# Rows of seven experts through DRAM and indirect DMA, in a two-layer decoder with top-2 experts

## The chip, the core and the metric

The kernel runs on one core of a Trainium2 chip, in one launch. The core's engines run side by side, each with its own queue of instructions in program order, and wait for each other by semaphores: TensorE multiplies matrices, VectorE and ScalarE work on rows and read TensorE's sums, GpSimd is a slower engine for the same kind of work, and SyncE does little but issue DMA transfers. The metric is the device time of one execution in microseconds, lower is better; 1471.25 us is the median of three runs before the change.

## What is computed

Two decoder layers over 256 tokens of 1024 numbers, in fp32. Each has a set of attention heads and then a feed-forward part: dense in layer 0, and in layer 1 two of eight experts for each token. A final RMSNorm ends it. The change lies in the experts and in the norm behind them:

```python
def _moe_swiglu(h, router, w1, w3, w2):
    logits = (xt @ router).astype(jnp.float32)
    top_v, top_i = lax.top_k(logits, TOP_K)            # TOP_K = 2 of 8 experts
    gates = jax.nn.softmax(top_v, axis=-1)
    ...
    def body(args):
        tok, g, e = args
        xb = xt[tok]                                   # the tokens of expert e
        y = (jax.nn.silu(xb @ w1[e]) * (xb @ w3[e])) @ w2[e]     # 1024 -> 3584 -> 1024
        return y * g[:, None].astype(y.dtype)
    ...
    out = jnp.zeros((t, d), h.dtype).at[row_tok].add(...)
...
x = x + _moe_swiglu(rmsnorm(x, ffn_norm[1]), ...)
return rmsnorm(x, final_norm)
```

## The kernel before

**Weights.** All weights come as one stream of 1 MB units, 128 rows of 2048 numbers (`Stream`). SyncE loads a unit into the next free buffer (`raw`); ScalarE copies each half (a piece) rounded to the matmul's format (`wh`, L305), VectorE computes the rest (`wl`, L306), and TensorE multiplies with both, so that a product is three matmuls (`mm3`, L454 to L456). Five split pieces of either kind exist; `split_to` keeps the splitting four pieces ahead of TensorE in the expert stage (`MAHEAD`). A buffer is loaded again once VectorE has split its second piece. Tiles of other stages are added as buffers when they are free (`widen`), and some are taken back (`retire`).

**Order.** The expert stage is written out by hand: each engine does its work in the order of the code. `get` hands out a split piece, splits the one four ahead and runs what was put off by `defer(n)` to the n-th piece from there.

**Routing.** `moe` transposes the token rows with TensorE (`natural`) and keeps them as a rounded part and a rest (`xnh`, `xnl`). From the router's products come rank, mask and `pos`, the place of each token among the tokens of each expert. 128 slots belong to an expert; if one has more tokens than that, a second pass follows the first, which the data here don't need.

**Experts.** `experts` runs 8 experts in 7 steps (e, j) of 512 hidden columns. A step is `g1` (two products with w1 and w3, bank `acc`) and `g2` of the step before (product with w2, bank `mm`); between them TensorE transposes the hidden tile `hd` in four pieces (`hidden`). Twelve pieces are used in a step. Around the steps stands what moves tokens to slots and back, all of it on TensorE with a one-hot matrix `oh` (slot by token):
- `gather`: 32 matmuls of 128x128 per expert, in step 5 of the expert before, in two groups; `gathered` takes them out of the bank with the norm's gains, in a rounded part (ScalarE) and a rest (VectorE).
- `back`: in step 6, two transposes of `oh` to `sT`, and the slots' 1/rms by two fp32 matmuls.
- `scatter`: in step 1 of the next expert, eight matmuls of 128x512 from `sT` and the two parts of the expert's output (`yh`, `yl`); `put` adds them to the token rows `x`, times the gate, on VectorE.

**The end.** `Final` norms the rows; its gains are spread over the 128 partitions by 16 small matmuls with 8 rows (`gains`, L1147), which TensorE does in the last step.

## Time and profile before

| what | value |
|---|---|
| median of the runs (lowest, highest) | 1471.25 us (1470.4, 1471.53) |
| the profiled execution, its span | 1470.91 us, 1468.7 us |
| TensorE busy | 1448.2 us, 99% |
| VectorE busy | 1225.0 us, 83% |
| ScalarE busy | 1047.2 us, 71% |
| GpSimd busy | 31.8 us, 2% |
| bytes moved | 426.36 MB, 290 GB/s over the span |
| the expert stage | from about 462 us to the end |

Busy time says how long an engine had an instruction in work, and matmuls overlap, so that 99% of TensorE's time is not 99% of its peak. The average hides stages too: in the expert stage VectorE and the DMA engines are much fuller than over the whole span. Times in the rows are counted from the span's start.

### The profile page before, as it was taken

To read this page: it belongs to the slowest core of one execution; us is meant where nothing else is said; L and a number is where in the kernel's file an instruction comes from. 1 tells how busy PE (TensorE), PEld (TensorE's weight loads), DVE (VectorE), ACT (ScalarE), POOL (GpSimd) and SP (SyncE) were. 2 spreads that over 40 slices of the span, in tenths; PEclk is the share of its full clock that TensorE was granted. 3 is DMA by queue.
4 is the path that set the end of the run, shared out by engine and by line. 5 is a ranking of instruction groups with operands and counts; after the bars stand their busy time and mean duration, and the time that the engine had idled before them with its cause. 6 is when DMAs were issued, how large, how long until landed. Compare 5 with 4: busy or idle time off the path is not lost.

```text
span 1468.7 us, 21467 instructions
## 1 busy us (share of the span) xinstructions
PE 1448.2 (99%) x8092; PEld 1253.7 (85%) x8092; DVE 1225.0 (83%) x1574; ACT 1047.2 (71%) x1387; POOL 31.8 (2%) x38
## 2 busy tenths in 40 slices
PE   9999999999999999999999999999999999999996
PEld 7999999999997888888888888888888888888885
DVE  6766656666756998999999999899999999989995
ACT  6665544455755877887877878778887877878884
POOL 2001000001000010000000000000000000000000
PEclk9999999999998999999999999999999999999998
DMA  9723555457437988999999999999999999999770
GB/s 367 297 87 121 189 183 177 154 192 249 142 145 292 358 319 321 357 371 339 355 362 366 346 358 360 343 359 365 347 361 354 378 332 355 372 346 358 247 254 31
DMA packets 62334, 426.36 MB, mean 290 GB/s; under 512 B 7176, under 2 KB 7824, under 8 KB 13712
## 3 DMA queue, kind: packets, MB, share of 16 engines
q1 hardware_dynamic: 62224, 424.92, 78.5%
q8 instruction: 65, 1.06, 0.3%
q14 instruction: 45, 0.37, 0.1%
HBM read 423.85 MB, written 1.05 MB: 289 GB/s over the span
## 4 chain that ended last, share of the span: by engine, by line
PE 96%; DVE 1%; ACT 1%; issue 1%; DMA 1%; SPq 0%; POOL 0%; ACTq 0%; DVEq 0%; POOLq 0%
PE acc L454 14%; PE acc L456 14%; PE acc L455 14%; PE mm L454 7%; PE mm L455 7%; PE mm L456 7%; PE B L972 3%; PE B L971 3%; PE B L970 3%; PE A L522 2%; PE A L523 2%; PE A L524 2%; PE tp L1187 2%; PE tp L1239 2%; PE A L594 2%; PE A L595 1%
## 5 line engine op out<-in xcount | busy, mean ns | idle before, releaser
L306 DVE TENSOR_TENSOR wl<-raw,wh 128x1024 fp32r<-128x1024 f32 (+2 forms) x801 | 966.8, 1224 | 140.9 <-ACT wh L305 103.5
L305 ACT ACTIVATE wh<-raw 128x1024 fp32r<-128x1024 f32 (+2 forms) x801 | 844.5, 1057 | 282.5 <-PE acc L456 105.3
L454 PE MATMUL acc<-wh,g 128*128 128x512 f32 x896 | 357.1, 399 | 0.0
L455 PE MATMUL acc<-wl,g 128*128 128x512 f32 x896 | 350.0, 391 | 0.4 <-DVE wl L306 0.4
L456 PE MATMUL acc<-wh,g 128*128 128x512 f32 x896 | 350.1, 391 | 0.0
L456 PEld LDWEIGHTS acc<-wh,g 128*128 128x128 f32 x896 | 168.6, 188 | 36.7
L455 PEld LDWEIGHTS acc<-wl,g 128*128 128x128 f32 x896 | 168.9, 189 | 33.6 <-DVE wl L306 0.9
L454 PEld LDWEIGHTS acc<-wh,g 128*128 128x128 f32 x896 | 168.6, 188 | 32.9
L454 PE MATMUL mm<-wh,th 128*128 128x512 f32 x440 | 171.9, 391 | 0.0
L455 PE MATMUL mm<-wl,th 128*128 128x512 f32 x440 | 171.7, 390 | 0.0
L456 PE MATMUL mm<-wh,tl 128*128 128x512 f32 x440 | 171.6, 390 | 0.0
L456 PEld LDWEIGHTS mm<-wh,tl 128*128 128x128 f32 x440 | 82.9, 188 | 17.6 <-DVE tl L460 0.3
L455 PEld LDWEIGHTS mm<-wl,th 128*128 128x128 f32 x440 | 82.9, 188 | 17.4
L454 PEld LDWEIGHTS mm<-wh,th 128*128 128x128 f32 x440 | 82.9, 188 | 17.3
L972 PE MATMUL B<-xh,wl 128*128 128x256 f32 x336 | 95.2, 283 | 0.0
L970 PE MATMUL B<-xh,wh 128*128 128x256 f32 x336 | 95.1, 283 | 0.0
L971 PE MATMUL B<-xl,wh 128*128 128x256 f32 x336 | 95.1, 283 | 0.0
L970 PEld LDWEIGHTS B<-xh,wh 128*128 128x128 f32 x336 | 64.5, 192 | 0.0
L971 PEld LDWEIGHTS B<-xl,wh 128*128 128x128 f32 x336 | 64.5, 192 | 0.0
L972 PEld LDWEIGHTS B<-xh,wl 128*128 128x128 f32 x336 | 64.5, 192 | 0.0
L594 PE MATMUL A<-xh,wh 128*128 128x256 f32 x176 | 51.4, 292 | 0.0
L595 PE MATMUL A<-xl,wh 128*128 128x256 f32 x176 | 49.7, 283 | 0.0
(256 smaller groups left out, 1749.3 us busy)
## 6 DMA issues: line engine op xcount, KB each, us to landing
raw<-in_wmoe SPq DMA_DIRECT2D x324, 1024.0 KB, 6.9
raw<-in_wt SPq DMA_DIRECT2D x53, 1024.0 KB, 4.8
raw<-in_wmoe SPq DMA_DIRECT2D x24, 512.0 KB, 5.3
ac<-in_att SPq DMA_DIRECT2D x2, 1728.0 KB, 8.8
raw<-in_wt SPq DMA_DIRECT2D x5, 512.0 KB, 4.8
raw<-in_wt SPq DMA_DIRECT2D x2, 960.0 KB, 16.1
raw<-in_wt SPq DMA_DIRECT2D x2, 928.0 KB, 8.4
raw<-in_wt SPq DMA_DIRECT2D x2, 832.0 KB, 8.8
```

The lines of the kernel that those rows point to most:

```text
L305: nc.scalar.activation(h[:, sl], raw[:, sl], AF.Copy)
L306: nc.vector.tensor_sub(l[:, sl], raw[:, sl], h[:, sl].bitcast(F32))
L454: pe.matmul(o, lh, rh, start=start, stop=False, **kw)
L455: pe.matmul(o, lh, rl, start=False, stop=False, **kw)
L456: pe.matmul(o, ll, rh, start=False, stop=stop, **kw)
L522: pe.matmul(o, wh[wsl], h, start=s0, stop=False, skip_group_check=True)
L523: pe.matmul(o, wh[wsl], lo, start=False, stop=False, skip_group_check=True)
L594: pe.matmul(o, hv[:, k], xh[:, k], start=k == 0, stop=False)
L595: pe.matmul(o, hv[:, k], xl[:, k], start=False, stop=False)
L970: pe.matmul(o, hv[:, k], xh[:, k], start=k == 0, stop=False)
L971: pe.matmul(o, hv[:, k], xl[:, k], start=False, stop=False)
L972: pe.matmul(o, lv[:, k], xh[:, k], start=False, stop=k == KC - 1)
```

## The change

Experts 1 to 7 get their tokens by another way, and the outputs of experts 0 to 6 go back by another way; expert 0 still gathers with matmuls, and expert 7 still scatters with them.

- **There.** The token rows `xx`, now in plain fp32, are multiplied by the norm's gains on GpSimd and written to DRAM (`x_out`, `x_rows`, 1 MB). For each expert two fp32 matmuls of the one-hot with two columns (`numbers`) give each slot's token number and 1/rms; GpSimd clears a tile and fetches the slots' rows by an indirect DMA with these numbers (`fetch`). TensorE turns the fetched rows with eight transposes (`turn`), which are split on their way out of the bank (`turned`).
- **Back.** ScalarE copies an expert's output to a tile that GpSimd writes to DRAM (`put`, `y_rows`, 512 KB). In step 1 of expert 7 GpSimd clears two tiles and fetches for each token the rows of its two places (`collect`, four indirect DMAs of 512 KB); a token with no place in experts 0 to 6 gets nothing by the bounds check. VectorE adds them, times the shares, in steps 3 and 4 of expert 7 (`add`). The places and shares come from `places`, 15 small VectorE instructions in step 1 of expert 0.
- **Else.** Gains of the MoE norm and of the final norm are loaded as rows spread over the partitions, so `Final.gains` and its matmuls go. One weight buffer more (`more`) stays to the end, and `oTh`, `oTl` are taken back at step 5 of expert 6. The two parts `xnh`, `xnl` and their subtractions go.

```diff
-ONCE = ("g1", "yy", "xx")
-RETIRE = {1: "g1", 2: "xx", 3: "yy"}
+ONCE = ("g1", "yy")
+RETIRE = {1: "g1", 3: "yy"}
+FAR = 4096.0
...
-        st.widen([big_slot("oTh"), big_slot("oTl")])
+        for tag in ("oTh", "oTl"):
+            st.widen([big_slot(tag)], tag)
         for tag in ONCE:
             st.widen([mp_slot(tag)], tag)
+        st.widen([mp_slot("more")])
+        row = mp.tile([128, D], F32, name="row")
+        nc.sync.dma_start(row, bcast(P_MOE, D))
...
-        def natural_x():
-            xx = mp.tile([128, 2, D], F32, name="xx")
+        def x_out():
+
             for t in range(2):
-                x.append(xx[:, t])
-                pool.tensor_add(x[t], xnh[t].bitcast(F32), xnl[t].bitcast(F32))
-
+                xg = mp.tile([128, D], F32, name="xg")
+                pool.tensor_mul(xg, x[t], row)
+                pool.dma_start(x_rows[128 * t:128 * t + 128], xg)
+
+        x_out()
...
-            def gains(self, c):
-                for i in range(4):
-                    pe.matmul(self.gf[c][:, 128 * i:128 * i + 128],
-                              ident[0:8, 4 * c + i:4 * c + i + 1].to_broadcast([8, 128]), self.gfin, start=True, stop=True)
...
                 p = bank()
-                for v in (xnh, xnl):
-                    for c, k in enumerate(ks):
-                        for t in range(2):
-                            pe.matmul(p[:, 128 * c:128 * c + 128], v[t][:, 128 * k:128 * k + 128], self.oh[t],
-                                      start=v is xnh and c == t == 0, stop=v is xnl and k == ks[-1] and t == 1,
-                                      skip_group_check=True)
+                for c, k in enumerate(ks):
+                    for t in range(2):
+                        pe.matmul(p[:, 128 * c:128 * c + 128], x[t][:, 128 * k:128 * k + 128], self.oh[t],
+                                  start=c == t == 0, stop=k == ks[-1] and t == 1, skip_group_check=True)
...
+            def numbers(self):
+                self.p = tp()
+                for t in range(2):
+                    pe.matmul(self.p[:, 0:2], self.oh[t], num[:, t], start=t == 0, stop=t == 1)
+
+            def numbered(self):
+                self.rsl = ms.tile([128, 1], F32, name="rsl", bufs=2)
+                self.who = ms.tile([128, 1], I32, name="who", bufs=2)
+                dve.tensor_scalar(self.who, self.p[:, 0:1], FAR, None, op0=ALU.add)
+                dve.tensor_copy(self.rsl, self.p[:, 1:2])
+
+            def fetch(self):
+
+                self.xg = mp.tile([128, D], F32, name="xg")
+                pool.memset(self.xg, 0.0)
+                pool.indirect_dma_start(self.xg, None, x_rows, bass.IndirectOffsetOnAxis(ap=self.who, axis=0),
+                                        bounds_check=S - 1, oob_is_err=False)
+
+            def turn(self, q):
+                self.p = tp()
+                for c in range(4):
+                    pe.transpose(self.p[:, 128 * c:128 * c + 128],
+                                 self.xg[:, 512 * q + 128 * c:512 * q + 128 * c + 128], ident)
...
-                    for c in range(2):
-                        sl = slice(512 * c, 512 * c + 512)
-                        st.defer(1 + c, lambda sl=sl, c=c: split_evac(yh[:, sl], yl[:, sl], Y[e][c]))
+                    ys = mp.tile([128, D], F32, name="yy")
+
+                    def put(c):
+                        act.activation(ys[:, 512 * c:512 * c + 512], Y[e][c], AF.Copy)
+                        if c == 1:
+                            pool.dma_start(y_rows[128 * e:128 * e + 128], ys)
+                    for c in range(2):
+                        st.defer(1 + c, lambda c=c: put(c))
...
+            def collect():
+
+                for t in range(2):
+                    yg.append(big.tile([128, 2, D], F32, name="yg", tag=("oTh", "oTl")[t]))
+                    pool.memset(yg[t], 0.0)
+                    for r in range(2):
+                        pool.indirect_dma_start(yg[t][:, r], None, y_rows,
+                                                bass.IndirectOffsetOnAxis(ap=take[:, r, t:t + 1], axis=0),
+                                                bounds_check=(E - 1) * 128 - 1, oob_is_err=False)
+
+            def add(t, r):
+                dve.scalar_tensor_tensor(x[t], yg[t][:, r], share[:, r, t:t + 1], x[t], op0=ALU.mult, op1=ALU.add)
...
-                if e and j == 1:
-                    for k in range(4):
-                        (b if k < 2 else c)[(0, 2, 0, 2)[k]] = [later(scatter, e - 1, k // 2, [k % 2], 1)]
...
+                if (e, j) == (E - 1, 1):
+                    c[1] = [collect]
+                if e == E - 1 and j in (3, 4):
+                    for r in range(2):
+                        (b, c)[r].setdefault(1, []).append(later(add, j - 3, r))
+                if half == 0 and (e, j) == (E - 2, 5):
+                    st.retire("oTh")
+                    st.retire("oTl")
...
-                if e + 1 < E and j == 4:
+                if e + 1 < E and j == 1:
                     st.defer(1, later(prepare, e + 1))
+                if e + 1 < E and j == 2:
+                    b[0] = [lambda: (G[e + 1].numbers(),
+                                     st.defer(1, lambda: (G[e + 1].numbered(), G[e + 1].fetch())))]
                 if e + 1 < E and j == 5:
                     for q in range(2):
-                        ks = list(range(4 * q, 4 * q + 4))
-                        b[2 * q] = [later(lambda ks: (G[e + 1].gather(ks, tp),
-                                                      st.defer(1, later(G[e + 1].gathered, ks))), ks)]
-                if e + 1 < E and j == 6:
+                        b[2 * q] = [later(lambda q: (G[e + 1].turn(q), st.defer(1, later(G[e + 1].turned, q))), q)]
+                if e == E - 2 and j == 6:
                     b[0] = [lambda: (G[e + 1].back(), st.defer(1, G[e + 1].backed))]
```

Three places show it in the order of the instructions. First TensorE in step 1 of expert 1, where a half of the scatter of expert 0 stood (`acc` and `mm` are the banks of the products, `tp` the bank for transposes, `g`, `th`, `tl` the slots' tokens and the hidden tile). Before:

```order
L455 MATMUL acc<-wl,g 128x512
L456 MATMUL acc<-wh,g 128x512
L1292 MATMUL tp<-yy,sT 128x512 x2
L454 MATMUL acc<-wh,g 128x512
L455 MATMUL acc<-wl,g 128x512
```

After the change, in step 5 of expert 0, where 16 gather matmuls stood in a row:

```order
L458 MATMUL acc<-wl,g 128x512
L459 MATMUL acc<-wh,g 128x512
L1250 MATMUL tp<-cst,xg 128x128 x4
L457 MATMUL acc<-wh,g 128x512
L458 MATMUL acc<-wl,g 128x512
```

The scatter's rows have gone without a row in their place, and a group of 16 gather matmuls has become one row of four transposes of the fetched tile.

Second, VectorE at the end of step 5 of expert 0 (`wl` are the splits of weights, `hd` and `tl` belong to the hidden tile, `g` are the rests of the gathered tokens). Before:

```order
L460 TENSOR_TENSOR tl<-tp,th 128x512
L306 TENSOR_TENSOR wl<-raw,wh 128x1024
L1199 SCALAR_TENSOR_TENSOR g<-tp,gains,g 128x128 x4
L306 TENSOR_TENSOR wl<-raw,wh 128x1024 x2
L1199 SCALAR_TENSOR_TENSOR g<-tp,gains,g 128x128 x4
L306 TENSOR_TENSOR wl<-raw,wh 128x1024
L1261 SCALAR_TENSOR_TENSOR hd<-acc,rsl,sg 128x512
```

After:

```order
L463 TENSOR_TENSOR tl<-tp,th 128x512
L309 TENSOR_TENSOR wl<-raw,wh 128x1024
L463 TENSOR_TENSOR g<-tp,g 128x512
L309 TENSOR_TENSOR wl<-raw,wh 128x1024 x2
L463 TENSOR_TENSOR g<-tp,g 128x512
L309 TENSOR_TENSOR wl<-raw,wh 128x1024
L1310 SCALAR_TENSOR_TENSOR hd<-acc,rsl,sg 128x512
```

Four instructions of 128x128 have become one of 128x512, twice, at the same place among the splits.

Third, GpSimd from the routing to the first experts (`rs_r` is the 1/rms, `xx` the token rows, `fm` the final norm's). Before, this is all that it does to the end of the kernel:

```order
L450 TENSOR_TENSOR rs_r<-rs_m,half 128x2
L1111 TENSOR_TENSOR xx<-xnh_5394,xnl_5396 128x1024
L1111 TENSOR_TENSOR xx<-xnh_5395,xnl_5397 128x1024
L1165 TENSOR_TENSOR fm<-fm,half 128x1 x2
L1371 TENSOR_LOAD cmaxi
```

After, up to the second expert's fetch:

```order
L453 TENSOR_TENSOR rs_r<-rs_m,half 128x2
L1119 TENSOR_TENSOR xg<-xx,row 128x1024
L1120 DMA x_rows<-xg 128x1024
L1119 TENSOR_TENSOR xg<-xx,row 128x1024
L1120 DMA x_rows<-xg 128x1024
L1243 MEMSET xg 128x1024
L1244 DMA xg<-x_rows,who 128x1024
L1332 DMA y_rows<-yy 128x1024
L1243 MEMSET xg 128x1024
L1244 DMA xg<-x_rows,who 128x1024
```

Clear, fetch and write-out repeat for each expert, seven times in all, in one queue.

## Rows read from the trace of the kernel before

**Rows 1.** The page: the span, and the chain that ended last by engine.
```profile
span 1468.7 us, 21467 instructions
...
PE 96%; DVE 1%; ACT 1%; issue 1%; DMA 1%; SPq 0%; POOL 0%; ACTq 0%; DVEq 0%; POOLq 0%
```

**Rows 2.** Table by stretches: start of the stage, a plain step, one expert.
```profile
core 0: us, PE busy (x) PEld busy (x) DVE busy (x) ACT busy (x) POOL busy (x), PEclk, DMA share, GB/s
462.00:482.00 20.00, 19.44 (x87) 15.81 (x87) 14.56 (x23) 16.34 (x20) 0.00 (x0) 0.94 0.78 262
...
587.00:604.00 17.00, 17.00 (x79) 14.00 (x78) 16.21 (x16) 14.47 (x17) 0.00 (x0) 1.00 1.00 374
...
710.00:833.00 123.00, 123.00 (x576) 102.31 (x575) 114.89 (x115) 98.60 (x109) 0.00 (x0) 1.00 0.97 357
```

**Rows 3.** Waits of SyncE's queue, then ScalarE's largest: total us, times, longest.
```profile
SPq L292 <- DVE wl L306: 792.8, 317, 9.2
...
ACT wh L305 <- PE acc L456: 78.5, 247, 0.8
```

**Rows 4.** The chain that ended last, steps around expert 1: start us, us, what.
```profile
551.21 1.73 PE tp L1187 x16
...
569.81 0.44 PE tp L1239 x4
...
571.87 0.34 PE tp L1207 x4
...
587.30 0.44 PE tp L1239 x4
...
604.12 0.44 PE tp L1239 x4
...
605.95 0.47 PE tp L1292 x2
...
622.75 0.44 PE tp L1239 x4
```

**Rows 5.** The same chain at the first gather group of expert 7.
```profile
1294.34 1.73 PE tp L1187 x16
```

**Rows 6.** The same chain in the last step, around the final gains.
```profile
1437.78 1.98 PE acc L1147 x16
...
1443.62 0.43 PE mm L455
...
1444.29 0.23 PE mm L454
```

**Rows 7.** Table by stretches: behind the final gains, and the gather of expert 0.
```profile
1440.50:1444.00 3.50, 3.50 (x10) 2.72 (x9) 2.05 (x3) 1.06 (x1) 0.00 (x0) 0.51 0.00 0
...
455.00:460.00 5.00, 4.74 (x23) 4.77 (x23) 3.03 (x12) 2.05 (x8) 0.70 (x1) 0.50 1.02 429
```

**Rows 8.** The chain in the gather of expert 0.
```profile
457.20 1.71 PE mm L1187 x8
```

**Rows 9.** VectorE's groups from 710 to 833 us, by shape: busy us, mean ns.
```profile
L1296 DVE SCALAR_TENSOR_TENSOR xx<-tp,gate,xx 128x512 f32<-128x512 f32 x4 | 3.0, 746 | 0.0
...
L1199 DVE SCALAR_TENSOR_TENSOR g<-tp,gains,g 128x128 fp32r<-128x128 f32 x8 | 2.3, 343 | 1.0 <-ACT g L1197 1.0
...
L460 DVE TENSOR_TENSOR yy<-mm,yy 128x512 fp32r<-128x512 f32 x2 | 1.4, 684 | 0.0
```

**Rows 10.** Order in time, VectorE before and during GpSimd's additions: start us, us.
```profile
491.48 9.16 DVE L306 TENSOR_TENSOR wl<-raw,wh 128x1024 fp32r<-128x1024 f32 x8
...
506.85 14.28 DVE L306 TENSOR_TENSOR wl<-raw,wh 128x1024 fp32r<-128x1024 f32 x8
...
513.15 5.76 POOL L1111 TENSOR_TENSOR xx<-xnh,xnl 128x1024 f32<-128x1024 f32 x2 [56.14 <-DVE wl L306]
```

**Rows 11.** DMA issues of the expert weights: count, KB each, us to landing.
```profile
raw<-in_wmoe SPq DMA_DIRECT2D x324, 1024.0 KB, 6.9
...
raw<-in_wmoe SPq DMA_DIRECT2D x24, 512.0 KB, 5.3
```

**Rows 12.** Order in time, one of VectorE's tiny instructions in `gates`.
```profile
478.31 0.17 DVE L1123 TENSOR_REDUCE gmx<-gate 128x2 f32<-128x16 f32 x1
```

**Rows 13.** Table by stretches: 5 us with a queue of loads to work off.
```profile
540.00:545.00 5.00, 5.00 (x24) 4.14 (x23) 5.00 (x6) 4.11 (x4) 0.00 (x0) 1.00 1.01 428
```

More of the change, by code (lines that the diff above doesn't have):

```diff
@@ L1098, in moe @@
         rs = rsqrt(ss, D, 2)
+        num = ms.tile([128, 2, 2], F32, name="num")
+        dve.tensor_copy(num[:, :, 0], ids[:, 0:2])
+        dve.tensor_copy(num[:, :, 1], rs[:, 0:2])
         cmax = ms.tile([128, 1], F32, name="cmax")
@@ L1125, in gates, with places @@
             dve.tensor_tensor(gate, gate, gm[:, 1, :, None].to_broadcast([128, 2, E]), op=ALU.mult)
+        take = ms.tile([128, 2, 2], I32, name="take")
+        share = ms.tile([128, 2, 2], F32, name="share")
+        def places():
+            n = E - 1
+            w = [ms.tile([128, 2, n], F32, name=f"pl{i}") for i in range(3)]
+            sm = ms.tile([128, 2, 2], F32, name="plm")
+            dve.tensor_tensor(w[0], pos[:, :, :n], ids[:, None, 2:2 + n].to_broadcast([128, 2, n]), op=ALU.add)
+            dve.tensor_scalar(w[1], pos[:, :, :n], -0.5, None, op0=ALU.is_gt)
+            dve.scalar_tensor_tensor(w[1], pos[:, :, :n], 127.5, w[1], op0=ALU.is_lt, op1=ALU.mult)
+            for r in range(2):
+                dve.scalar_tensor_tensor(w[2], rank[:, :, :n], float(r), w[1], op0=ALU.is_equal, op1=ALU.mult)
+                g = ms.tile([128, 2, n], F32, name="plg", bufs=2)
+                dve.tensor_mul(g, w[2], gate[:, :, :n])
+                dve.tensor_reduce(share[:, r], g, AX, ALU.add)
+                dve.tensor_mul(w[2], w[2], w[0])
+                dve.tensor_reduce(sm[:, r], w[2], AX, ALU.add)
+            far = ms.tile([128, 2, 2], F32, name="plf")
+            dve.tensor_scalar(far, sm, 0.5, FAR, op0=ALU.is_lt, op1=ALU.mult)
+            dve.scalar_tensor_tensor(take, sm, -1.0, far, op0=ALU.add, op1=ALU.add)
         psx.close()
@@ L1135, in moe, with __init__ @@
         class Final:
-            def __init__(self, gfin):
-                self.gfin = gfin
-                self.gf = [acc() for c in range(2)]
+            def __init__(self):
                 self.ss = ms.tile([128, 4], F32, name="fss")
@@ L1177, in __init__, with place @@
                 self.oh = oh or onehot(e)
-                both = mp.tile([128, 2, KC, 128], F32R, name="g", tag=f"g{e % 2}")
+                self.tag = f"g{e % 2}"
+            def place(self):
+                both = mp.tile([128, 2, KC, 128], F32R, name="g", tag=self.tag)
                 self.gh, self.gl = both[:, 0], both[:, 1]
@@ L1202, in back, with turned @@
+            def turned(self, q):
+                if q == 0:
+                    self.place()
+                split_evac(self.gh[:, 4 * q:4 * q + 4], self.gl[:, 4 * q:4 * q + 4],
+                           self.p.rearrange("p (c t) -> p c t", c=4))
             def back(self):
-                p = tp()
+                self.p = tp()
                 for t in range(2):
-                    pe.transpose(p[:, 128 * t:128 * t + 128], self.oh[t].bitcast(F32), ident)
-                for t in range(2):
-                    pe.matmul(p[:, 256:257], self.oh[t].bitcast(F32), rs[:, t:t + 1], start=t == 0, stop=t == 1)
@@ L1304, in prepare @@
                 G[e] = Slots(e)
+            yg = []
+            def collect():
[8 more added lines that the diff above has]
+                dve.scalar_tensor_tensor(x[t], yg[t][:, r], share[:, r, t:t + 1], x[t], op0=ALU.mult, op1=ALU.add)
             G[0] = Slots(0, oh0 if half == 0 else None)
-            for i in range(4):
-                ks = [2 * i, 2 * i + 1]
-                G[0].gather(ks, (tp, mm)[i % 2])
-                G[0].gathered(ks)
             if half == 0:
-                st.defer(8, gates)
+                G[0].place()
+                for i in range(4):
+                    ks = [2 * i, 2 * i + 1]
+                    G[0].gather(ks, (tp, mm)[i % 2])
+                    G[0].gathered(ks)
+                st.defer(8, gates)
+                st.defer(12, places)
+            else:
+                places()
+                G[0].numbers()
+                G[0].numbered()
+                G[0].fetch()
+                for q in range(2):
+                    G[0].turn(q)
+                    G[0].turned(q)
             for i, (e, j) in enumerate(steps):
@@ L1341, in experts @@
                     st.ahead = TAHEAD
-                    fin = Final(gfin)
-                    b[2] = [later(fin.gains, 0), later(fin.gains, 1)]
+                    fin = Final()
+                    fin.row = final_row
                     c[1] = [later(hidden, e, j)]
```

60 lines of the change are left out of this document (26 added, 34 removed).

## The prediction

> **What bounds the kernel now.** I read the page first: of the chain that ended last, 96% is TensorE work [rows 1]. Next, the table by stretches, for the expert stage. Over one expert (710 to 833 us) TensorE is busy for all 123.00 us, VectorE for 114.89, ScalarE for 98.60, and the DMA engines have a share of 0.97 at 357 GB/s [rows 2]. Three of the four are near full, so the question is which of them waits for which. The waits tell: SyncE, which issues the weight loads, stood 792.8 us waiting for VectorE's split of an earlier piece, that is, for a free buffer; and the waits of ScalarE, the first reader of a weight, are for TensorE to release a split buffer, with no row that names a DMA (the largest is shown) [rows 3]. So loads run ahead of use, and TensorE sets the pace, with VectorE some 7% behind it. What leaves TensorE's queue is worth its full length, until VectorE or the loads become the limit.
>
> How long things take on TensorE I read from the chain, where a row's length is the distance to the next. A step of the expert loop begins with four transposes of the hidden tile. A plain step lasts 604.12 - 587.30 = 16.82 us; the step with the way back (`back`) 587.30 - 569.81 = 17.49; the step with the scatter 622.75 - 604.12 = 18.63; a group of 16 gather matmuls takes 1.73, and there are two per expert [rows 4]. From the first group of expert 1, at 551.21, to that of expert 7, at 1294.34, are six experts: a period of 123.9 us [rows 4, 5].
>
> **The change on TensorE.** *Gather, experts 1 to 7.* Twice 1.73 us go. In their place stand twice four transposes of the fetched rows, the same operation and shape as the hidden tile's four, 0.44 [rows 4]. Saved: 2 x (1.73 - 0.44) = 2.58 an expert, 7 x 2.58 = 18.1 us.
>
> *Scatter, experts 0 to 6.* Eight matmuls go and nothing replaces them on TensorE: 18.63 - 16.82 = 1.81 an expert, 7 x 1.81 = 12.7 us. Expert 7 keeps its own.
>
> *`back`.* It costs 17.49 - 16.82 = 0.67, of which the two fp32 matmuls with one column (four records, so an fp32 matmul is two) are 0.34 [rows 4]. They stay, with two columns, as `numbers`; the two transposes stay for expert 7 alone. I take 0.23 an expert for them, 7 x 0.23 = 1.6 us.
>
> *Final gains.* Sixteen matmuls of 1.98 us go, and more with them: behind them the chain has nine 512-column matmuls at 0.43 us where one at full clock takes 0.23 [rows 6], and the granted clock is 0.51 in that stretch, which is the level of 1.2 GHz [rows 7]. These sixteen, with 8 of the 128 rows in use, are all that TensorE did differently before it fell, so I let the loss go too: 1.98 + 9 x 0.20 = 3.8 us (bounds 2.0, if the clock falls for another reason, and 3.8).
>
> *Gather of expert 0.* It stays on TensorE, as 16 fp32 matmuls. At two records each these are 32, as many as the 32 now, which take 1.71 us for eight [rows 8] with the clock at 0.50 [rows 7]. I take no difference; an fp32 record could cost half or one and a half times as much, so the bounds are -3.4 and +3.4 of its 6.8 us.
>
> Sum: 18.1 + 12.7 + 1.6 + 3.8 = 36.2 us less on TensorE; 2.58 + 1.81 + 0.23 = 4.6 us an expert make the period 119.2 instead of 123.9.
>
> **What hides the rest, and what it costs.** *VectorE.* It loses the four adds of the scatter (3.0 us an expert), the rests of `yy` (1.4) and the eight rests of the gather (2.3) [rows 9], and gains two 128x512 rests (1.4, the form of `yy`) and two tiny ones: 114.89 x 123.9 / 123 - 6.7 + 1.7 = 110.7 of the new 119.2. It stays behind TensorE, with 8.5 us an expert to spare.
>
> *GpSimd* was nearly empty; now it clears a tile, starts an indirect fetch and writes the outputs out, for every expert. No row shows a clear or a transfer of GpSimd's. The nearest are its two 128x1024 additions, 5.76 us together; while they ran, eight of VectorE's splits took 14.28 us, where eight took 9.16 a step earlier: VectorE lost 5.1 us [rows 10]. Per expert the bounds are then nothing and three such operations, 3 x 5.1 / 2 = 7.7 us of VectorE, which fits into the 8.5. I take nothing, since two of the three only start transfers and the third has no input. The Trainium skill ("SBUF — State Buffer", SBUF: two separate sides) says that a VectorE instruction with two inputs in SBUF contends with a GpSimd instruction that reads SBUF; these rows agree (splits with two inputs, an addition that reads, 5.1 us lost), and by it the clear, which reads nothing, would cost nothing, which no run here shows. The sum is the same by both.
>
> *Waiting for the fetch.* Expert e + 1 gets its numbers in the second half of step 2 of expert e; its rows are turned in the second half of step 5: 3 x 16.82 = 50 us in between. TensorE's next work is queued in order behind the turn, so a late fetch would stop everything. A 1 MB weight load lands 6.9 us after issue [rows 11] and a GpSimd operation is about 2.9; fetch, with half a megabyte, I put at 10 to 15 us. Hidden by 35.
>
> *The start.* Two multiplications on GpSimd (`x_out`) replace the two additions, but now while the first weights of the stage are split, and `places` puts 15 tiny VectorE operations, some 0.17 us each by the like one of `gates` [rows 12], 2.6 us, into the second step. 5.1 + 2.6 = 7.7 us more there; VectorE has 20 - 14.56 = 5.4 us free between 462 and 482 [rows 2]. What is over, 2.3 us, I charge as 2 (bounds 0 and 7.7, all of it exposed).
>
> *The end.* Four additions of 128x1024 on VectorE in steps 3 and 4 of expert 7, about twice 746 ns each [rows 9], 6 us, replace 28 of half that size earlier. VectorE has 17 - 16.21 = 0.8 us free in a plain step [rows 2], and splits run four pieces ahead of TensorE, 12 pieces to 16.82 us, that is 5.6 us. I take 0 (bounds 0 and 4).
>
> *The load path.* Weights are 324 x 1024 + 24 x 512 KB [rows 11] = 352.3 MB, 44.0 MB an expert. Two half-megabyte trips per expert add 1.05: 45.1 MB in 119.2 us, 378 GB/s. A plain step ran at 374 at a share of 1.00 [rows 2], which looks like a ceiling; but the 5 us from 540, with a queue to work off, show 428 [rows 13]. I take the latter as the ceiling, at 88% use. The Trainium skill ("DMA: Bandwidth & Descriptors", Specifications) gives about 358 GB/s as the HBM limit of a core, by which the new demand would not be met and the change would lose time. The trace goes over that figure, with 374 in 17 us and 428 in 5 [rows 2, 13].
>
> The profiled execution took 1470.9 us, 0.3 below the median of the runs; 1470.9 - 36.2 + 2 = 1436.7, so **1437**.
>
> **Rivals.** *A: the loads bind at 374 GB/s*, the rate of a plain step. 45.1 MB / 374 = 120.6 us an expert, 1.4 over; 7 x 1.4 = 10: **1447**. For it: the share is already 1.00 in that row. Against: 428 with a backlog, and SyncE waiting for buffers, not for the engines.
>
> *B (slower): loads bind at 357 GB/s*, the rate of the whole expert, if its share of 0.97 means that the engines have no more to give over a long stretch [rows 2]. 45.1 MB / 357 = 126.3 us an expert, 7.1 over, 50 us: **1487**. The 374 and the 428 [rows 2, 13] speak against it, but they are short. The rule of the Trainium skill above comes to the same case.
>
> *C: the fetch starves (slower).* If GpSimd gets at SBUF only between VectorE's splits, and needs it row by row, 128 waits of 1.15 us (9.16 / 8, [rows 10]) make 147 us, 97 more than the 50: 7 x 97 = 679, **2116**. It decides from (36.2 - 2) / 7 = 4.9 us late, a fetch of 55 us or 48 such waits. For it: VectorE is 93% busy and the two engines did disturb each other. Against: one GpSimd operation got through in 2.9 us amid the splits.
>
> *D: GpSimd takes VectorE's spare time and more.* Three operations an expert at 4 us of VectorE each are 12, 3.5 over the 8.5: 7 x 3.5 = 25, **1462**.
>
> *E: nothing moves*, because the breaks that gather and scatter gave VectorE and the loads were needed: **1471**. Against: the plain steps, without breaks, run at 16.82 one after another.
>
> **How the numbers follow.** Forecast 0.68 (its own spread 1431 to 1446, from the bounds above), A 0.12, D 0.07, E 0.03, B 0.04, C 0.06. The range takes in the forecast and A with a part of the forecast's own spread above it: 1430 to 1452. Faster by over 0.2% (about what a measurement of this kernel can tell from no change): 0.68 + 0.12 + 0.07 = 0.87; within: 0.03; slower: 0.10.
>
> **What would show it.** Right: equal expert periods of about 119.2 us with TensorE busy throughout; turn rows of 0.44; no TensorE wait for the fetched tile; VectorE near 111 us a period; over 375 GB/s held for whole periods; a granted clock of 1.00 up to the last step. Wrong: ScalarE waiting for a weight load (A, B); TensorE waiting for the fetched rows (C); splits stretched to 2 us and more around GpSimd's work, with TensorE waiting for them (D); a first stretch more than 4 us longer than now (my 2 for the start).

## The result, and the profile after

| | us |
|---|---|
| before, median of 4 runs | 1470.91 (1470.4 to 1471.53) |
| changed kernel, median of 4 runs | 1435.33 (1434.78 to 1435.99) |
| ratio, with 95% interval | 0.9758 [0.9741, 0.9775] |
| profiled execution before: time, span | 1470.91, 1468.7 |
| profiled execution after: time, span | 1435.42, 1433.4 |

Faster by 2.4%. The forecast was 1437. The page of the changed kernel, where [rows 1] stood: the span is 35.3 us shorter, and the chain that ended last is still TensorE's.

```profile
span 1433.4 us, 20931 instructions
...
PE 95%; DVE 2%; DMA 1%; ACT 1%; issue 0%; SPq 0%; POOL 0%; POOLq 0%; DVEq 0%; ACTq 0%
```

The chain through the expert steps, where [rows 4] and [rows 5] stood (start us, us, what):

```profile
550.64 0.44 PE tp L1288 x4
552.47 0.44 PE tp L1250 x4
568.40 0.44 PE tp L1288 x4
...
602.04 0.44 PE tp L1288 x4
618.85 0.44 PE tp L1288 x4
636.14 0.44 PE tp L1288 x4
...
1265.39 0.44 PE tp L1288 x4
...
1401.10 0.44 PE tp L1288 x4
1409.76 0.44 PE tp L1288 x4
```

L1288 is the hidden tile's turn that opens each step, L1250 the turn of the fetched rows (its other half follows at 555.66). The step with the two turns lasts 568.40 - 550.64 = 17.76, the one with `numbers` 636.14 - 618.85 = 17.29, every other 16.8. The step that had the scatter is a plain step now. Six periods from 550.64 to 1265.39 make 119.1 us each, against 123.9 before.

The table by stretches, with the columns of [rows 2]: the gather of expert 0 and its first products, one whole period, and the last step (where [rows 7] stood).

```profile
455.00:459.00 4.00, 3.92 (x34) 3.91 (x35) 2.40 (x13) 2.61 (x9) 0.69 (x1) 1.00 1.01 428
459.00:482.00 23.00, 21.04 (x96) 16.84 (x95) 21.15 (x29) 20.40 (x24) 6.90 (x4) 1.00 0.93 367
482.00:487.50 5.50, 2.97 (x13) 1.93 (x11) 5.12 (x19) 2.76 (x3) 0.95 (x1) 1.00 0.86 347
487.50:491.00 3.50, 3.50 (x9) 2.69 (x10) 3.50 (x4) 1.06 (x1) 0.00 (x0) 0.56 0.48 108
...
620.68:739.80 119.12, 119.12 (x548) 98.57 (x546) 111.53 (x105) 97.59 (x103) 3.18 (x3) 1.00 0.99 377
...
1402.00:1410.00 8.00, 8.00 (x40) 6.59 (x38) 6.95 (x7) 6.43 (x8) 0.00 (x0) 1.00 0.00 1
```

In a period TensorE is busy throughout, VectorE for 111.53 us, and 377 GB/s are held. The only new hole is at the start. Of the 23 us before 482 TensorE stands idle for 2.0, where it stood for 0.6 of 20 in [rows 2]; between 482 and 487.5 it works 2.97 of 5.5 us, and behind that the clock is down for 3.5 us. TensorE's waits say for what (total, times, longest):

```profile
PE mm L458 <- DVE wl L309: 2.4, 1, 2.4
...
PE acc L458 <- DVE wl L309: 1.3, 1, 1.3
```

The shorter one comes first and ends at 480.00, the longer one at 486.80 (starts of the two matmuls in TensorE's order in time).

Where the 35.3 us went, from chain row to chain row of the two profiles. Of the kernel before these are the first gather matmuls and the hidden tile's turns that open step 5 of expert 0, open the last step, and stand at its end:

```profile
455.26 1.94 PE tp L1187 x8
...
549.38 0.44 PE tp L1239 x4
...
1433.21 0.44 PE tp L1239 x4
...
1445.68 0.44 PE tp L1239 x4
```

Up to step 5 of expert 0 (549.38 before, 550.64 after) the kernel is 1.3 longer. From there to the last step (1433.21 before, 1401.10 after): 883.83 against 850.46, 33.4 less. The last step but its end (to 1445.68 before, 1409.76 after): 12.47 against 8.66, 3.8 less. The end: 23.0 against 23.6. Together 1.3 - 33.4 - 3.8 + 0.6 = -35.3.

### The profile page after: what moved, and what is told of

Read it like the earlier page. It is cut to its first block, busy times and chain, and to the rows that moved or that the text cites. A ratio compares the mean times of both kernels' runs of the same rounds, so it can differ in the third digit from the quotient of the medians.

```text
span 1433.4 us, 20931 instructions
## 1 busy us (share of the span) xinstructions
PE 1408.8 (98%) x7838; PEld 1216.7 (85%) x7838; DVE 1200.5 (84%) x1516; ACT 1036.2 (72%) x1338; POOL 65.5 (5%) x67
## 4 chain that ended last, share of the span: by engine, by line
PE 95%; DVE 2%; DMA 1%; ACT 1%; issue 0%; SPq 0%; POOL 0%; POOLq 0%; DVEq 0%; ACTq 0%
PE acc L457 14%; PE acc L459 14%; PE acc L458 14%; PE mm L459 7%; PE mm L458 7%; PE mm L457 7%; PE B L976 3%; PE B L975 3%; PE B L974 3%; PE A L525 3%; PE A L526 2%; PE A L527 2%; PE tp L1288 2%; PE A L597 2%; PE A L598 1%; PE A L599 1%
```

## Experiments

All start from the changed kernel. They ran in three groups, each with its own runs of the kernel before on the same chip as the base of the ratios; that base was 1470.46 to 1470.61 in the median. Differences to the changed kernel are to its 1435.33.

### One part undone: the gather, the scatter, the final gains

**The gather goes back to TensorE** (no rows to DRAM, no multiplications for them on GpSimd, no fetch; `numbers` for the slots' 1/rms alone, in step 6):

```diff
-        x_out()
...
-                    b[0] = [lambda: (G[e + 1].numbers(),
-                                     st.defer(1, lambda: (G[e + 1].numbered(), G[e + 1].fetch())))]
...
-                        b[2 * q] = [later(lambda q: (G[e + 1].turn(q), st.defer(1, later(G[e + 1].turned, q))), q)]
+                        ks = list(range(4 * q, 4 * q + 4))
+                        b[2 * q] = [later(lambda ks: (G[e + 1].gather(ks, tp),
+                                                      st.defer(1, later(G[e + 1].gathered, ks))), ks)]
```

> The changed kernel with one part undone: experts 1 to 7 gather with 16 fp32 matmuls each again (32 records), nothing is written to or fetched from DRAM on the way there; the way back through DRAM stays. Theory T, TensorE sets the pace and each instruction there is worth its length: 7 x 2.6 = 18 us more than the changed kernel's 1435.3, less 2 to 4 us of its loss in the first steps, since GpSimd's two multiplications go: 1449 to 1452. Rival V, VectorE sets the pace: the rests of the gather cost it 2.3 us an expert instead of 1.4, 7 x 0.9 = 6 us: about 1441, less what the start gives back.

Measured: 1451.16 us (1450.4 to 1453.12), ratio 0.9868 [0.9853, 0.9883], 15.8 more than the changed kernel. Its chain shows the gather again, as rows of 16 records (eight fp32 matmuls), and the period between two of them:

```profile
551.16 1.78 PE tp L1212 x16
...
672.93 1.78 PE tp L1212 x16
```

121.8 us, 2.65 over the changed kernel's 119.1; the prediction had 2.58. TensorE's length decides; VectorE, busy for 110.85 of the 120 us from 720 in that run, has much the load that it has in the changed kernel. Seven times 2.65 is 18.5, though, and 15.8 were measured; the 2.7 between them are put down to the start, which has no multiplications here.

**The scatter goes back to TensorE** (outputs stay on the chip and are split, `scatter` in step 1 of the next expert, `back` for every expert; `places`, the four fetches at the end and their additions go):

```diff
-                    ys = mp.tile([128, D], F32, name="yy")
...
+                    yy = mp.tile([128, 2, D], F32R, name="yy")
+                    yh, yl = yy[:, 0], yy[:, 1]
...
+                if e and j == 1:
+                    for k in range(4):
+                        (b if k < 2 else c)[(0, 2, 0, 2)[k]] = [later(scatter, e - 1, k // 2, [k % 2], 1)]
...
-                if e == E - 2 and j == 6:
+                if e + 1 < E and j == 6:
```

> The other part undone: the outputs of experts 0 to 6 are scattered by matmuls again, with the transposes for them; tokens still reach experts 1 to 7 through DRAM. Theory T: 12.7 + 1.6 us more than 1435.3, less 1 to 3 us, since the 15 small VectorE instructions leave the first steps: 1446 to 1449. Rival V: VectorE has 3.0 + 1.4 us an expert more and 6 us fewer in expert 7: 7 x 4.4 - 6 = 25 more, 1460.

Measured: 1447.19 us (1445.02 to 1450.28), ratio 0.9838 [0.9823, 0.9853], 11.9 more. The scatter is in the chain again (four rows of 0.47 and 0.45), with a period of 725.81 - 604.68 = 121.1:

```profile
604.68 0.47 PE tp L1341 x2
...
725.81 0.47 PE tp L1341 x2
```

2.0 over 119.1, where the prediction had 1.81 + 0.23 = 2.04 for scatter and `back`. The two undone parts together make 4.65 of the 4.7 us by which the periods of the two kernels differ, which leaves at most 0.1 to the additional weight buffer; that was not undone by itself. Here 7 x 2.0 = 14.0 stand against 11.9: the 2.1 between them are put down to `places` and the additions at the end, which are gone.

**The sixteen gain matmuls go back into the last step:**

```diff
+            def gains(self, c):
+                for i in range(4):
+                    pe.matmul(self.gf[c][:, 128 * i:128 * i + 128],
+                              ident[0:8, 4 * c + i:4 * c + i + 1].to_broadcast([8, 128]), self.gfin, start=True, stop=True)
...
+                    b[2] = [later(fin.gains, 0), later(fin.gains, 1)]
```

> The changed kernel with the 16 small matmuls that spread the final gains put back in the last step. Theory T with the clock: 1.98 us for them and 1.8 for nine matmuls at the lower clock behind them, 3.8 in all: 1439.1, and the granted clock near 0.5 for 3.5 us behind them. Rival: the clock fell there for another reason; then 2.0 us more, 1437.3, and either no fall or one that the changed kernel has too.

Measured: 1437.25 us (1436.18 to 1439.38), ratio 0.9778 [0.9764, 0.9791], 1.9 more in the median: the matmuls alone, without a loss of clock. The chain and the table by stretches of its profile, of a run of 1437.25, say so:

```profile
1405.61 1.98 PE acc L1180 x16
```

```profile
1405.50:1415.00 9.50, 9.50 (x52) 8.04 (x52) 7.57 (x8) 5.61 (x8) 0.00 (x0) 1.00 0.00 0
```

The same 1.98 us of matmuls, and a granted clock of 1.00 (2.4 GHz) over and behind them, where [rows 7] had 0.51 (1.2 GHz). So they don't always bring the clock down. Two of the five runs, with 1438.4 and 1439.38, come near theory T's 1439.1; whether the clock fell in those no trace shows.

### The start of the stage: late_both, late_places, plain_rows

The changed kernel's hole from 478.7 to 491 us has two suspects, seen in VectorE's order in time, and GpSimd's below it (start us, us, engine, what; in brackets what ended the idle time before):

```profile
466.00 6.58 DVE L309 TENSOR_TENSOR wl<-raw,wh 128x1024 fp32r<-128x1024 f32 x4 [0.16 <-ACT wh L308]
...
476.31 2.49 DVE L1091 TENSOR_SCALAR oh<-cst,pos,mask 128x128 f32<-128x128 f32 x2
...
482.22 0.97 DVE L1146 TENSOR_SCALAR pl<-pos 128x14 f32<-128x14 f32 x1
...
485.44 0.16 DVE L1158 SCALAR_TENSOR_TENSOR take<-plm,plf 128x4 int32<-128x4 f32 x1
```

```profile
464.99 3.12 POOL L1119 TENSOR_TENSOR xg<-xx,row 128x1024 f32<-128x1024 f32 x1 [8.15 <-DMA row<-in_par]
...
476.07 2.39 POOL L1119 TENSOR_TENSOR xg<-xx,row 128x1024 f32<-128x1024 f32 x1 [6.86 <-DMA x_rows<-xg]
...
482.21 0.95 POOL L1243 MEMSET xg<- 128x1024 f32 x1 [2.84 <-DMA x_rows<-xg]
```

Four splits take 6.58 us instead of 4.6: the first of them, beside GpSimd's multiplication, takes 3.18 and the others the usual 1.21. Two `oh` take 2.49, where the same two took 0.60 at 598.87 with no multiplication beside them. TensorE's wait of 1.3 us, which ends at 480.00, lies behind these and ahead of `places`. The 15 operations of `places` stand in one piece from 482.14 to 485.6, the second of them stretched to 0.97 by the clear that starts with it.

**Both moved into the steps of expert 0** (the load of the gains' row moves with `x_out`):

```diff
-        x_out()
...
-                st.defer(12, places)
...
+                if half == 0 and i == 1:
+                    x_out()
+                if half == 0 and (e, j) == (0, 4):
+                    st.defer(1, places)
```

> The changed kernel with two things of its start moved: the row of gains is loaded, and the token rows multiplied on GpSimd and written out, from step 1 of expert 0 on instead of before step 0, and the 15 small VectorE instructions (places and shares) come in step 4 instead of step 1. Theory S: TensorE's wait of 2.4 us for a split near 485 us, and the lower clock behind it (1.4 us), come from VectorE being held up by GpSimd and by these instructions in the same 20 us; both go, 1431.5. Rival: the wait comes from the three loads of ScalarE's function tables there, which stay: 1435.

Measured: 1431.81 us (1428.64 to 1434.02), ratio 0.974 [0.9727, 0.9754]. The start can be had for 3.5 us less. The second multiplication met VectorE again, and this time it was GpSimd that stood:

```profile
490.22 9.11 POOL L1119 TENSOR_TENSOR xg<-xx,row 128x1024 f32<-128x1024 f32 x1 [6.27 <-DMA x_rows<-xg]
```

```profile
487.90 9.15 DVE L309 TENSOR_TENSOR wl<-raw,wh 128x1024 fp32r<-128x1024 f32 x8
```

Eight splits at their usual 1.14 us, and one multiplication of 9.11 instead of 2.4 to 3.1. The split behind them took 2.82, as the first one beside the other multiplication did with 2.83.

**Only `places` moved:**

```diff
-                st.defer(12, places)
...
+                if half == 0 and (e, j) == (0, 4):
+                    st.defer(1, places)
```

> Half of late_both: only the 15 small operations that make the slots move, from the second step of expert 0 to step 4; the multiplications of GpSimd stay at the start. Theory M (multiplications are the larger part: eight splits stretched by about 2 us, hot rows by 1.9): gains 1 to 1.5 us of the 4.9, 1433.8 to 1434.5. Rival P (the small operations, which stretch from 482 to 485.6 right where TensorE waits 2.4 and 1.3 us, are the larger part): gains the 3.5 us of late_both, 1431.8.

Measured: 1432.24 us (1431.7 to 1435.21), ratio 0.9743 [0.973, 0.9756]: 3.1 less than the changed kernel, close to rival P by the median. The runs reach from P to beyond M, and the profiled one is the slowest of them, with 1435.21. It still has a hole, without `places`: TensorE waits 2.4 us for the hidden tile up to 481.51, behind three splits that take 5.70 us instead of 3.5 beside the second multiplication (the third 3.42 by itself).

```profile
PE tp L1288 <- DVE hd L1310: 2.4, 1, 2.4
...
471.95 5.70 DVE L309 TENSOR_TENSOR wl<-raw,wh 128x1024 fp32r<-128x1024 f32 x3 [0.44 <-ACT wh L308]
```

The profile of scatter_back, which has no `places` either, shows the same wait. So the multiplications can open such a hole by themselves, and which of the two is the larger part of the loss stays open: leaving out `places` gave 3.1 here and 2.1 in scatter_back, leaving out the multiplications 2.7 in gather_back.

**And the multiplications taken away** (x goes out as it is, and the gains are applied to the turned rows):

```diff
-                xg = mp.tile([128, D], F32, name="xg")
-                pool.tensor_mul(xg, x[t], row)
-                pool.dma_start(x_rows[128 * t:128 * t + 128], xg)
+                pool.dma_start(x_rows[128 * t:128 * t + 128], x[t])
...
-                split_evac(self.gh[:, 4 * q:4 * q + 4], self.gl[:, 4 * q:4 * q + 4],
-                           self.p.rearrange("p (c t) -> p c t", c=4))
+                self.gathered(list(range(4 * q, 4 * q + 4)))
```

> Start of the stage, cause GpSimd's multiplications: x goes to DRAM as it is, without the two 128x1024 multiplications by the gains and the load of their row; the gains are applied to the turned rows instead, as expert 0 does it; the 15 small operations of the slots are in step 4 of expert 0 as in the run late_both. Theory M (these multiplications and VectorE's splits hold each other up, wherever they stand): nothing of GpSimd's two is left beside the splits, and the products of expert 0 run without a pause; start loss of the changed kernel (4.9 us by its trace against the kernel before) all but gone: 1435.3 - 4.9 = 1430.4, so 1429 to 1431.5, no slower than late_both (1431.8). Rival P (only the placing of the small operations counts, the multiplications were covered anyway): the same as the run late_places of this job, within 1 us.

Measured: 1430.37 us (1428.28 to 1430.76), ratio 0.9726 [0.9713, 0.9739], the fastest of all: 5.0 less than the changed kernel, of which 1.9 lie between this run and late_places. Its start, by stretches:

```profile
459.00:482.00 23.00, 22.44 (x103) 18.33 (x103) 19.41 (x31) 20.37 (x24) 0.30 (x1) 1.00 0.95 378
482.00:487.50 5.50, 5.50 (x26) 4.53 (x26) 5.50 (x7) 5.24 (x6) 0.00 (x0) 1.00 1.01 399
```

The hole is gone. From the gather's first matmul to step 5 this profile takes 89.0 us, 6.4 less than the changed kernel's (starts of the matmuls, 455.29 to 544.32 against 455.08 to 550.48), at a clock of 1.00 in both gathers. The runs of late_places lie 3.5 apart, more than the 1.9 between its median and this one, so the size of that difference, not its sign, is uncertain.

### Rival D: pool_work and pool_spread

```diff
+                if half == 0 and e + 1 < E and j == 3:
+                    a[0] = [lambda: [pool.tensor_sub(row, row, row) for _ in range(6)]]
```

> GpSimd gets six additional subtractions of 128x1024 (two inputs in SBUF) per expert for experts 0 to 6, in step 3, with no reader: 42 more operations. Theory D (VectorE is held up by each, as by the two additions of the kernel before, 5.1 us for two): VectorE's 111.5 us per period become 111.5 + 6 x 2.55 = 126.8, 7.7 over the 119.1 of the period: 7 x 7.7 = 54, 1489. Theory G (whoever comes second waits, and under VectorE's steady load this is GpSimd): each takes 3 to 9 us on GpSimd, VectorE's spare of 7.6 us takes what is left: 1435 to 1437.

Measured: 1474.18 us (1472.37 to 1474.74), ratio 1.0025 [1.0014, 1.0036], 38.9 more than the changed kernel: all of the gain lost, and neither number met. Orders in time of GpSimd, VectorE and TensorE in one period, and that period in the table by stretches:

```profile
631.04 16.34 POOL L1416 TENSOR_TENSOR row<-row 128x1024 f32<-128x1024 f32 x6
```

```profile
637.06 11.41 DVE L309 TENSOR_TENSOR wl<-raw,wh 128x1024 fp32r<-128x1024 f32 x4
```

```profile
640.02 0.50 PE L458 MATMUL acc<-wl,g 128*128 128x512 f32 x1 [1.16 <-DVE wl L309]
...
642.86 0.50 PE L458 MATMUL acc<-wl,g 128*128 128x512 f32 x1 [1.17 <-DVE wl L309]
```

```profile
629.40:753.90 124.50, 120.26 (x545) 98.33 (x544) 119.22 (x105) 97.70 (x103) 19.16 (x9) 1.00 0.94 358
```

Here the two engines took turns: four splits in 11.41 us, one every 2.85 instead of 1.14, and a subtraction every 2.72. VectorE's busy time grew by 119.22 - 111.53 = 7.7 us, 1.3 per subtraction and not 2.55. That is what it had to spare in a whole period, and yet the period grew by 124.5 - 119.1 = 5.4. TensorE uses a split piece every 16.82 / 12 = 1.40 us; at one per 2.85 the pieces that were split ahead lasted from 631.04 to 640.02 - 1.16 = 638.86, 7.8 us, and from then on it waited, with the pieces it waited for 642.86 - 640.02 = 2.84 apart.

The next run was to spread the six over six steps:

```diff
+                if half == 0 and e + 1 < E and j < 6:
+                    a[0] = [lambda: pool.tensor_sub(row, row, row)]
```

> The same six additional subtractions on GpSimd per expert as in the run pool_work, but one in each of steps 0 to 5 instead of all six in step 3. In pool_work each cost VectorE 1.3 us (119.2 us a period instead of 111.5), 7.7 in sum, as much as its spare time; TensorE nevertheless lost 5.4 us a period. Theory L (the loss came from their standing together: 7.7 us at one place is more than the lead of the splits, 5.6 us, while one of 1.3 a step is taken up): 1435 to 1442. Theory P (the spare time of VectorE is used up, wherever they stand): 1465 to 1475, as in pool_work.

Measured: 1464.1 us (1463.2 to 1464.97), ratio 0.9953 [0.9936, 0.997]. It doesn't tell L from P as it was meant to, because the six were not spread. Nothing holds such an operation back to its step, and GpSimd, which stands waiting for the numbers of the next fetch, ran five in a row once that wait was over, and the sixth at 731.81:

```profile
632.30 1.63 POOL L1244 DMA_INDIRECT xg<-x_rows,who  x1 [20.73 <-DVE rsl L1238]
633.96 13.51 POOL L1416 TENSOR_TENSOR row<-row 128x1024 f32<-128x1024 f32 x5
```

```profile
642.93 0.50 PE L458 MATMUL acc<-wl,g 128*128 128x512 f32 x1 [1.16 <-DVE wl L309]
```

Still, five in a row and one apart cost 755.37 - 632.30 - 119.1 = 4.0 us a period, six in a row 5.4, with the first wait again 642.93 - 1.16 - 633.96 = 7.8 us after the first subtraction. The one that stands apart stretches a split to 3.03 us, and TensorE waits for nothing behind it, which speaks against P; that six truly apart cost nothing was not tried.

### Rival C: fetch_8us and fetch_17us

The numbers and the fetch are put closer to the turn: half a step ahead, and one step ahead, instead of three.

```diff
-                if e + 1 < E and j == 2:
-                    b[0] = [lambda: (G[e + 1].numbers(),
+                if e + 1 < E and j == 5:
+                    a[0] = [lambda: (G[e + 1].numbers(),
```

> Numbers and fetch of the next expert only half a step (8.4 us) ahead of the turn, instead of three steps (50 us). Theory T (a fetch needs 12 to 14 us: 0.34 for the numbers on TensorE, VectorE's queue in front of the two small copies, 1.6 on GpSimd, 9.1 from issue to landing): late by 4 to 6 us each time, and all of TensorE's queue behind it: 7 x 4 to 6 = 28 to 42 us more, 1463 to 1477. Rival (TensorE is not stopped by a late fetch because other work stands ahead of the turn, or the fetch is under 8 us): 1435 to 1437. Rival C's size (55 us and more): over 1750.

Measured: 1488.21 us (1485.98 to 1490.35), ratio 1.0117 [1.0101, 1.0132], 52.9 more. TensorE's total wait for the seven fetches, and the stretch of one wait and the one behind it:

```profile
PE tp L1250 <- DMA xg<-x_rows,who: 40.1, 7, 6.1
```

```profile
551.00:562.00 11.00, 4.91 (x25) 3.92 (x24) 5.50 (x5) 4.58 (x6) 1.88 (x1) 0.88 1.00 372
562.00:567.00 5.00, 5.00 (x18) 3.93 (x17) 1.91 (x2) 1.85 (x3) 0.00 (x0) 0.59 0.19 79
```

Numbers at 548.34 on TensorE, copies on VectorE at 550.77 (behind VectorE's splits), start of the fetch at 551.77, landing 9.1 us after that: 12.5 us in all. TensorE waits 40.1 / 7 = 5.7 us for each. That part is as expected. The rest of the 52.9 / 7 = 7.6 us per expert is the clock: behind the pause it is mostly at the lower level of 1.2 GHz, 0.59 on the mean of 5 us, which costs 2.

```diff
-                if e + 1 < E and j == 2:
+                if e + 1 < E and j == 4:
```

> Numbers and fetch one step (16.8 us) ahead of the turn, instead of three (50 us). In the run fetch_8us it was 12.6 us from the numbers on TensorE (548.34) to the landing (560.9). Theory T: 12.6 is hidden by 16.8, TensorE waits for no fetched row: 1434 to 1437. Rival (how long a fetch takes varies with the loads in front of it, by more than 4 us): a wait at some experts, each with the loss of clock behind it, 1440 to 1455.

Measured: 1435.48 us (1435.29 to 1435.97), ratio 0.976 [0.9743, 0.9776]: no loss. A fetch needs more than 8.4 us and less than 16.8, and the kernel gives it 50.

### Rivals A and B: extra_writes4 and extra_writes8

More writes to DRAM per expert, with no reader (four here, eight in the second):

```diff
+        z_rows = dram.tile([4 * 128, D], F32, name="z_rows")
...
+                            for z in range(4):
+                                pool.dma_start(z_rows[128 * z:128 * z + 128], ys)
```

> Four more writes of 512 KB to DRAM per expert for experts 0 to 6, with no reader: 2.1 MB on top of 45.1, in a period of 119.1 us a demand of 396 GB/s instead of 379. Theory T (the load path has room up to the 428 GB/s of the short stretch): 1435 to 1437. Theory A' (the path is full at the share of 0.99 that the changed kernel shows, about 380): 47.2 MB / 380 = 124.2 us a period, 7 x 5.1 = 36 more: 1471.

> Eight more writes of 512 KB per expert for experts 0 to 6: 4.2 MB on top of 45.1, a demand of 414 GB/s. Theory T (room up to 428): 1435 to 1440. Theory A' (full at about 380): 49.3 MB / 380 = 129.7 us a period, 7 x 10.6 = 74 more: 1509. In between, the rate at which the time begins to grow is the limit of the path.

Measured: 1434.95 us (1433.68 to 1438.92), ratio 0.9762 [0.9744, 0.9781], and 1435.02 us (1434.58 to 1435.46), ratio 0.9757 [0.9741, 0.9774]. Both are the changed kernel's time. With four writes a period runs at 396 GB/s; with eight, in the table by stretches:

```profile
739.80:858.90 119.10, 119.10 (x545) 98.55 (x545) 111.52 (x105) 97.59 (x103) 7.21 (x11) 1.00 1.01 415
```

415 GB/s over a whole period at a share of 1.01, where the kernel before showed 1.00 at 374. The weight loads land later, in the median after 10.3 us instead of the changed kernel's 7.2, and the period is no longer for it.

## Why the prediction was right, and which of its steps were not

**Gather, scatter and `back`: right.** 32.4 us were summed, and the stretch that holds them became 33.4 shorter; the two runs that undo one part each give 2.65 and 2.0 us per expert for 2.58 and 2.04. The turns last 0.44 as the hidden tile's do.

**VectorE: right.** 110.7 us a period were worked out, 111.53 measured. It stays behind TensorE, and the clear costs the splits nothing, as the order in time of VectorE and of GpSimd shows (three splits before a clear 1.24 each, four beside one 1.25):

```profile
595.23 3.73 DVE L309 TENSOR_TENSOR wl<-raw,wh 128x1024 fp32r<-128x1024 f32 x3
598.87 0.60 DVE L1091 TENSOR_SCALAR oh<-cst,pos,mask 128x128 f32<-128x128 f32 x2
599.38 5.02 DVE L309 TENSOR_TENSOR wl<-raw,wh 128x1024 fp32r<-128x1024 f32 x4
```

```profile
600.61 0.98 POOL L1243 MEMSET xg<- 128x1024 f32 x1
```

**The load path: right.** The ceiling was put at 428 by a stretch of 5 us; 377 was needed and 415 is had. A and B fall: the share of 1.00 in [rows 2] was not a full path. The figure of about 358 GB/s by which the Trainium skill came to B's case has a condition in another of its pages ("Perfetto Trace Analysis", Roofline): it is a core's share when both cores of a pair draw on the memory, and one core alone may reach some 120% of it. This kernel runs on one core, and the trace agrees: 415 is 116%.

**Waiting for the fetch: right.** 10 to 15 us were put down, and 12.5 measured where it shows.

**The final gains: the size right, the cause half wrong.** 3.8 us were taken and 3.8 came. But 1.8 of it was the clock, charged to the sixteen matmuls because nothing else differed ahead of its fall; in the profile with them put back the clock stayed at 1.00, and in the median they cost 1.9. The lower bound of the prediction, 2.0, is what the change brings by itself there. What brought the clock down in that stretch of the kernel before stays open.

**The gather of expert 0: right at the same clock, but the profile differs.** It took 455.08 to 458.93, 3.9 us, where the kernel before took 7.1. That is not the change: the matmul rows of the changed kernel, and of fetch_8us, which has the same instructions up to there, are (min/median/max ns)

```profile
L1215 PE MATMUL tp<-oh,xx x16: 275/275/347, 455.1 to 457.7; 128*128 128x128 f32 x16
```

```profile
L1215 PE MATMUL tp<-oh,xx x16: 421/421/553, 454.4 to 459.4; 128*128 128x128 f32 x16
```

the first at a granted clock of 1.00 (2.4 GHz) in 455 to 460 us, the second at 0.50 (1.2 GHz), as in [rows 7], where such a record of the kernel before takes 415. So an fp32 record costs what an fp32r record cost, as assumed, and 3.2 us of the profile's gain is the clock of that execution. Another 1.0 is the clock right behind the gather, where five matmuls of the kernel before, from 462.32 to 464.51, still ran at 0.54 and took 2.19 us, for 0.23 each at full clock.

**The start: the step that failed.** 2 us were charged, and the hole cost about 5: from the gather's first matmul to the row where the periods begin it was 94.1 us before and is 95.6 now, though 3.2 us of clock in the gather and 0.2 of `back` went, which makes 4.9 (5.9 with the clock behind the gather). The medians say the same: without `places` and without the multiplications (plain_rows) it is 5.0 less. The step took the idle time of VectorE between 462 and 482 as cover for the multiplications and the 15 small operations together. Between 459 and 482 VectorE is now busy for 21.15 of 23 us: the multiplications hold up a split and an `oh` by some 2 us each, and TensorE waits 1.3 for it already there. The small operations come behind that stretch, in one piece, with the split pieces used up; 3.5 us of VectorE in one piece there are 2.4 us of waiting on TensorE, and the clock behind that is mostly at 1.2 GHz (0.56 over 3.5 us, a loss of 1.5). Idle time earlier is no cover later; what is split ahead is. The bounds, 0 to 7.7, held the loss. One of the small ones was also stretched by the clear, to 0.97 us from the 0.17 that it takes in late_both. The prediction weighed the Trainium skill's rule on instructions with two inputs, by which a clear costs nothing; the same page has a second one ("SBUF — State Buffer", Who interferes with whom): a `tensor_scalar` can run in a mode that takes the shared port pair, and then it contends with any GpSimd instruction. The trace agrees with both, with 0.97 for the `tensor_scalar` and undisturbed splits beside a clear.

**The end:** 0 was taken, 0.6 measured, within its bounds.

**The sum.** That the forecast came within 2 us of the median is luck in part: some 3 us too little for the start and 3 us and more of clock in and behind the gather, which the sum did not have, nearly cancel in the profiles. Without that clock the stretch up to step 5 would be more than 4 us longer than before, which the prediction names as a sign of being wrong.

**Rival D** is a real danger, priced too high for one operation (1.3 us of VectorE, not 4) and too mildly for many: it compared a period's sum with a period's spare time, and pool_work lost 5.4 us a period with the spare time just covering it. The changed kernel shows none of this in its periods: VectorE's 111.53 us are 0.8 over the sum that put nothing down for GpSimd.

## What to carry to other kernels

When one engine is busy all the time, its time falls by the length of what leaves its queue, read from chain row to chain row, as long as each new helper is checked by its own resource: a queue for time to landing, the path for bytes. Judge cover at the place where the new work stands, by what is prepared ahead there (four pieces at most in this kernel, 4 x 1.40 = 5.6 us of TensorE's work), not by an engine's idle time in the whole period or in the stretch before. A DMA share of 1.00 didn't say here that the path was full; the rate with a backlog, 428 GB/s, was the better guide to the 415 that could be had.

## What was not expected of the hardware

- The gather of expert 0 in its changed form ran at granted clocks from 0.50 to 1.00 (455 to 460 us) in different executions, with the same instructions up to there in the changed kernel (1.00) and fetch_8us (0.50), worth up to 3.2 us. Ahead of it, from 450 to 455 us, TensorE was busy for 2.37 us in the one and 2.29 in the other. What decides was not found; runs of one kernel that differ by 3 to 5 us (late_both: 1428.64 to 1434.02) may be this.
- A pause of TensorE of 6 us costs more than its length: the granted clock was 0.59 over the next 5 us, about 2 us lost.
- VectorE's splits and GpSimd's operations with two inputs, side by side, show three outcomes: a split stretched (3.18 us instead of 1.21), turns (one split every 2.85 us, one subtraction every 2.72), or GpSimd held up behind a row of splits that keep their pace (9.11 us for one multiplication).
- An indirect fetch of 128 rows of 4 KB lands 9.1 us after its start in the median of the changed kernel's seven, with the load path at a share of 0.99; GpSimd is busy with it for 1.6 us. In late_both, beside a row of splits, it was busy once for 7.54.
